# Gates of a two-block transformer kernel: products of two groups of tokens in one go, comparisons issued on their own

## The chip, the cores and the metric

The kernel runs on one core of a Trainium2 chip. The metric is the device time of one execution in microseconds (us), and the time before is the median of three runs. A core has a matrix engine (TensorE, PE in the profile; its weight loads are a row of their own, PEld), a vector engine (VectorE, DVE), an activation engine (ScalarE, ACT), a general engine (GpSimd, POOL) and a queue that issues transfers (SyncE, SP). They run side by side, each through its own instructions in program order, and wait for each other through semaphores.

## The reference

Two transformer blocks run on 256 tokens of width 1024. The change lies in the last part of the second block, a mixture of 16384 very small experts. Per token, 8 heads choose 16 experts each, so 128 experts, with gates from a softmax:

```python
i1 = jnp.take_along_axis(i_top[:, :, 0], c_idx // PEER_TOPK, axis=-1)
i2 = jnp.take_along_axis(i_top[:, :, 1], c_idx % PEER_TOPK, axis=-1)
expert = i1 * N_KEYS + i2
gates = jax.nn.softmax(c_score, axis=-1)
...
a = jax.nn.gelu(jnp.einsum('td,thkd->thk', xb, u).astype(jnp.float32), approximate=False)
w = (gb * a).astype(xb.dtype)
```

An expert is a pair (i1, i2) of 128 keys each. Instead of gathering the rows of the chosen experts, the kernel computes the activation of all 16384 experts for all tokens and multiplies it by a gate that is zero where an expert wasn't chosen. For a token the 128 x 128 gates are the sum over its 128 choices of gate x onehot(i1) x onehot(i2), which is a matrix product with the choices on the contracted axis.

## The kernel before, in words

`Builder` writes the instructions of all engines in one pass. Weights come as 533 units of 128 x 1024 floats (512 KB), each loaded by SP into one of three raw buffers (`load`) and split by `prefetch` into a high part `hi` (ACT, L169) and a rest `lo` (DVE, L170), so that a product takes three matmuls, high by high, high by low and low by high.

The stage concerned is the loop over the 128 units `pu` in `peer`. For each, `f_tile` (L324) makes 24 matmuls of 256 columns into one of two PSUM banks `mm` (lines L332 to L334), with a call of `tick(1.3, False)` after 12 of them and of `tick(1.3)` at the end. Between the last matmul and the second tick it calls the unit's `evac`, `evu`: a gelu on ACT of the tokens whose gates aren't there yet, straight into X (L1488), and for the tokens whose gates are there a gelu on ACT in PSUM (L1490) and a multiplication on DVE into X (L1491), which holds the gates. The second tick also splits one more unit (L169, L170). A bank `mm` is free for the next unit but one when its L1491 is done.

Order of the work around the change: `tick` takes 1.3 from the count of each side task, a Python generator, and runs it on while that count is not positive; what the generator yields is added to the count. `gates` is such a task. A bare yield of it stands for 3.3, so that a group of four tokens falls on every second or third tick. There are 64 groups. For one group `hot` writes, for each of the four tokens, `m1` (a comparison of the row 0 to 127 with the first key of each choice, POOL, L1375), `oh` = `m1` times the gate's high part (ACT, L1377), `m2` = a comparison with the second key, scaled (DVE, L1378) and `ol` = `m1` times the gate's rest (DVE, L1380), all 128 x 128 in half precision; of each of the four tiles there are two buffers. The products are eight matmuls of 128 columns (L1388), per token one with `oh` and one with `ol`, into a PSUM bank `sd`, of which there are two in turn. The spread then takes the bank apart: for the units not yet multiplied (from `u_done` up) ACT copies the gates into X (L1396); for those already there DVE multiplies X by them (L1398), with tokens and units crossed.

In the kernel before, a step of the task issues the products of group g, then `hot(g + 1)`, then the spread of group g, and yields. `routing`, which comes ahead of it in the same task, makes the keys `kT`.

Of the kernel before, what the change touches and what calls it, by code (L numbers as in the profile page):

```python
# [8 lines left out]
F16 = mybir.dt.float16  # L9
I32 = mybir.dt.int32  # L10
U32 = mybir.dt.uint32
AF = mybir.ActivationFunctionType
OP = mybir.AluOpType
# [103 lines left out]
class Builder:  # L117
# [363 lines left out]
    def spread(self, hn, t, dst, col):  # L481
        self.transposes(hn[t].ap, t, dst, col)
        hn[t].free()
# [882 lines left out]
    def gates(self, kT, X):  # L1366

        nc = self.nc

        def hot(g):  # L1370
            tile = lambda name: self.pw.tile([128, 4, 128], F16, name=name, bufs=2)
            m1, m2, oh, ol = (tile(n) for n in ("m1", "m2", "oh", "ol"))
            key = lambda w, i: kT[:, w, 4 * g + i:4 * g + i + 1]
            for i in range(4):
                nc.gpsimd.tensor_scalar(m1[:, i], self.iota, key(0, i), None, op0=OP.is_equal)  # L1375
            for i in range(4):
                nc.scalar.activation(oh[:, i], m1[:, i], AF.Copy, scale=key(2, i))  # L1377
                nc.vector.tensor_scalar(m2[:, i], self.iota, key(1, i), 1.0 / self.SCALE, op0=OP.is_equal, op1=OP.mult)  # L1378
            for i in range(4):
                nc.vector.tensor_scalar(ol[:, i], m1[:, i], key(3, i), None, op0=OP.mult)  # L1380
            return (oh, ol), m2
        o = hot(0)
        yield
        for g in range(64):
            ps = self.sd()
            for i in range(4):
                for p in range(2):
                    nc.tensor.matmul(ps[:, i * 128:i * 128 + 128], o[0][p][:, i], o[1][:, i], start=(p == 0),  # L1388
                                     stop=(p == 1))
            if g < 63:  # L1390
                o = hot(g + 1)
            E = self.u_done
            pv = ps.rearrange("p (t i) -> p t i", t=4)
            x = X[:, :, 4 * g:4 * g + 4].rearrange("p i t -> p t i")
            if E < 128:
                nc.scalar.activation(x[:, :, E:128], pv[:, :, E:128], AF.Copy)  # L1396
            if E:
                nc.vector.tensor_mul(x[:, :, 0:E], pv[:, :, 0:E], x[:, :, 0:E])  # L1398
            self.g_done = 4 * g + 4
            yield  # L1400

    def peer(self):
        nc, hT = self.nc, self.uT
# [407 lines left out]
```

## Time and profile before

| what | us |
|---|---|
| median of 3 runs (lowest to highest) | 1655.06 (1654.47 to 1655.62) |
| the profiled execution, its own time | 1655.53 |
| its span in the profile | 1653.8 |
| PE busy in the span | 1632.5 |
| DVE busy | 1148.0 |
| ACT busy | 977.9 |
| POOL busy | 268.6 |
| POOL's comparisons L1375 alone, 256 of them | 233.2 |

The span is the time between the first and the last event of the profile; the profiled execution's own time has 1.7 us more around it. An engine's busy time is the time in which at least one of its instructions is under way; instructions of one engine overlap a little, so that the distance from one start to the next is often shorter than a duration. POOL's comparisons start between 1003.5 and 1283.9 us; that stretch is Gates.

### The profile page before, as it was taken

How to read it: one execution, taken by the hardware profiler on the slowest of the kernel's cores; microseconds unless marked ns; L12 is line 12 of the kernel's file. 1: busy time of each engine (PE TensorE's matmuls, PEld its weight loads, DVE VectorE, ACT ScalarE, POOL GpSimd, SP SyncE). 2: the span in 40 equal slices, each digit the busy share in tenths (PEclk: the TensorE clock that was granted, in tenths of full speed). 3: DMA queues.
4: the chain of work that ended last, by engine and by line, in shares of the span. 5: the costliest groups of instructions: out<-in, count | busy, mean ns of one | idle time of the engine just before them, and what ended most of it. 6: DMA issues, size and time to landing. Idle time of an engine off the chain costs nothing.

```text
span 1653.8 us, 29236 instructions
## 1 busy us (share of the span) xinstructions
PE 1632.5 (99%) x11102; PEld 1481.6 (90%) x11102; DVE 1148.0 (69%) x2366; ACT 977.9 (59%) x1826; POOL 268.6 (16%) x311
## 2 busy tenths in 40 slices
PE   8999999999999999999999999999999999999998
PEld 6999899988898899979889999999999888888886
DVE  6554765877756645487657998899999755555554
ACT  6443676786555544467355565888877555444454
POOL 0000000000000000000100003988888000000000
PEclk9999999999999999999999999999999999999999
DMA  7565643364524656555244555444454555555553
GB/s 280 192 208 175 227 143 116 115 202 143 179 103 154 216 190 206 177 185 197 78 140 143 192 190 192 166 163 164 161 166 153 180 205 194 194 195 193 191 191 128
DMA packets 79325, 288.77 MB, mean 175 GB/s; under 512 B 8784, under 2 KB 8912, under 8 KB 79056
## 3 DMA queue, kind: packets, MB, share of 16 engines
q1 hardware_dynamic: 77904, 281.66, 49.8%
q10 hardware_dynamic: 1280, 5.24, 1.0%
q8 instruction: 87, 1.43, 0.3%
q14 instruction: 54, 0.44, 0.1%
HBM read 285.82 MB, written 1.05 MB: 173 GB/s over the span
## 4 chain that ended last, share of the span: by engine, by line
PE 81%; DVE 11%; ACT 3%; issue 2%; DMA 2%; POOL 1%; SPq 0%; POOLq 0%; DVEq 0%; ACTq 0%
PE mm L332 12%; PE mm L334 12%; PE mm L333 12%; PE acc L349 10%; PE acc L351 10%; PE acc L353 10%; DVE lo L170 4%; PE mm L303 2%; PE mm L300 2%; PE mm L299 2%; DMA raw<-ws 2%; PE sd L1388 1%; ACT hi L169 1%; DVE m L1378 1%; DVE X L1260 1%
## 5 line engine op out<-in xcount | busy, mean ns | idle before, releaser
L170 DVE TENSOR_TENSOR lo<-raw,hi 128x1024 fp32r<-128x1024 f32 x414 | 506.6, 1228 | 237.5 <-ACT hi L169 236.1
L332 PE MATMUL mm<-uT,hi 128*128 128x256 f32 x2104 | 597.1, 284 | 2.1 <-DVE X L1491 1.7
L334 PE MATMUL mm<-uT,lo 128*128 128x256 f32 x2104 | 587.1, 279 | 0.0
L333 PE MATMUL mm<-uT,hi 128*128 128x256 f32 x2104 | 586.9, 279 | 0.0
L169 ACT ACTIVATE hi<-raw 128x1024 fp32r<-128x1024 f32 x414 | 436.3, 1058 | 214.9 <-PE acc L353 171.1
L332 PEld LDWEIGHTS mm<-uT,hi 128*128 128x128 f32 x2104 | 397.1, 189 | 4.9 <-DVE X L1491 2.6
L333 PEld LDWEIGHTS mm<-uT,hi 128*128 128x128 f32 x2104 | 397.1, 189 | 0.8
L334 PEld LDWEIGHTS mm<-uT,lo 128*128 128x128 f32 x2104 | 397.0, 189 | 0.0
L1375 POOL TENSOR_SCALAR m<-iota,kT 128x128 f16<-128x128 f16 x256 | 233.2, 927 | 197.8 <-DVE kT L1358 149.9
L438 POOL TENSOR_TENSOR hr<-hv,mhalf 128x1 f32<-128x1 f32 x26 | 14.4, 552 | 816.3 <-DVE hv L437 816.3
L349 PE MATMUL acc<-hi,wf 128*128 128x512 f32 x384 | 118.9, 390 | 0.0
L351 PE MATMUL acc<-lo,wf 128*128 128x512 f32 x384 | 118.7, 389 | 0.0
L353 PE MATMUL acc<-hi,wf 128*128 128x512 f32 x384 | 118.5, 389 | 0.0
L170 DVE TENSOR_TENSOR lo<-fa,hi 128x1024 fp32r<-128x1024 f32 x69 | 84.1, 1233 | 34.0 <-ACT hi L169 33.7
L531 ACT ACTIVATE fa<-mm 128x256 f32<-128x256 f32 x36 | 13.8, 383 | 122.9 <-PE mm L334 122.9
L351 PEld LDWEIGHTS acc<-lo,wf 128*128 128x128 f32 x384 | 72.1, 188 | 15.2
L353 PEld LDWEIGHTS acc<-hi,wf 128*128 128x128 f32 x384 | 72.1, 188 | 15.1
L349 PEld LDWEIGHTS acc<-hi,wf 128*128 128x128 f32 x384 | 72.1, 188 | 14.9
L1488 ACT ACTIVATE X<-mm 128x256 f32<-128x256 f32 (+40 forms) x126 | 39.6, 314 | 76.0 <-PE mm L334 75.0
L1377 ACT ACTIVATE oh<-m,kT 128x128 f16<-128x128 f16 x256 | 81.1, 390 | 0.0
L169 ACT ACTIVATE hi<-fa 128x1024 fp32r<-128x1024 f32 x69 | 70.7, 1051 | 5.6 <-PE mm L303 3.1
L1398 DVE TENSOR_TENSOR X<-sd,X 128x184 f32<-128x184 f32 (+31 forms) x64 | 60.9, 951 | 1.2 <-ACT X L1396 1.1
(364 smaller groups left out, 2550.9 us busy)
## 6 DMA issues: line engine op xcount, KB each, us to landing
raw<-ws SPq DMA_DIRECT2D x442, 512.0 KB, 3.3
fa<-ws SPq DMA_DIRECT2D x91, 512.0 KB, 4.4
fa<-rows ACTq DMA_DIRECT2D x5, 512.0 KB, 4.7
fa<-mem ACTq DMA_DIRECT2D x1, 1024.0 KB, 7.7
X<-keysT ACTq DMA_DIRECT2D x1, 1024.0 KB, 5.0
out<-X SPq DMA_DIRECT2D x4, 256.0 KB, 2.0
h<-x SPq DMA_DIRECT2D x2, 256.0 KB, 2.8
h<-x SPq DMA_DIRECT2D x1, 512.0 KB, 7.3
```

The lines of the kernel that those rows point to most:

```text
L169: nc.scalar.activation(hi, raw, AF.Copy)
L170: nc.vector.tensor_sub(lo, raw, hi.bitcast(F32))
L332: nc.tensor.matmul(ps, wh, ah[:, k, :], start=(k == 0), stop=False)
L333: nc.tensor.matmul(ps, wh, al[:, k, :], start=False, stop=False)
L334: nc.tensor.matmul(ps, wl, ah[:, k, :], start=False, stop=(k == 7))
L349: nc.tensor.matmul(o[h], ah[:, k, ts], hi[:, hs[h]], start=first, stop=False)
L351: nc.tensor.matmul(o[h], ah[:, k, ts], lo[:, hs[h]], start=False, stop=False)
L353: nc.tensor.matmul(o[h], al[:, k, ts], hi[:, hs[h]], start=False, stop=last)
L1375: nc.gpsimd.tensor_scalar(m1[:, i], self.iota, key(0, i), None, op0=OP.is_equal)
L1377: nc.scalar.activation(oh[:, i], m1[:, i], AF.Copy, scale=key(2, i))
L1398: nc.vector.tensor_mul(x[:, :, 0:E], pv[:, :, 0:E], x[:, :, 0:E])
L1488: nc.scalar.activation(X[:, i, g:256], ps[:, g:256], AF.Gelu)
```

## The change

The tiles of `hot` are the same, but its comparisons on POOL are a function of their own, `ones`, and the products and the spread of a group too. Two groups are made up at the start. Then a round takes two groups: the 16 matmuls of both, into both banks `sd`; the comparisons of the group after next; a yield of 1.3; the rest of that group's `hot` and the spread of the first group; the comparisons of the next one; a yield of 2.7; the rest of its `hot` and the spread of the second group; a yield of 2.6. The three yields together are 6.6, twice 3.3. The computation is the same.

```diff
-        def hot(g):
-            tile = lambda name: self.pw.tile([128, 4, 128], F16, name=name, bufs=2)
-            m1, m2, oh, ol = (tile(n) for n in ("m1", "m2", "oh", "ol"))
-            key = lambda w, i: kT[:, w, 4 * g + i:4 * g + i + 1]
+        tile = lambda name: self.pw.tile([128, 4, 128], F16, name=name, bufs=2)
+        key = lambda g, w, i: kT[:, w, 4 * g + i:4 * g + i + 1]
+
+        def ones(g):
+            m1 = tile("m1")
             for i in range(4):
-                nc.gpsimd.tensor_scalar(m1[:, i], self.iota, key(0, i), None, op0=OP.is_equal)
+                nc.gpsimd.tensor_scalar(m1[:, i], self.iota, key(g, 0, i), None, op0=OP.is_equal)
+            return m1
+
+        def hot(g, m1):
+            m2, oh, ol = (tile(n) for n in ("m2", "oh", "ol"))
             for i in range(4):
...
             return (oh, ol), m2
-        o = hot(0)
-        yield
-        for g in range(64):
+
+        def products(o):
             ps = self.sd()
             for i in range(4):
                 for p in range(2):
...
-            if g < 63:
-                o = hot(g + 1)
+            return ps
+
+        def spread(g, ps):
             E = self.u_done
...
             self.g_done = 4 * g + 4
-            yield
+        o = [hot(g, ones(g)) for g in range(2)]
+        yield
+        for g in range(0, 64, 2):
+            pss = [products(p) for p in o]
+            o = []
+            for i in range(2):
+                more = g + 2 + i < 64
+                if more:
+                    m1 = ones(g + 2 + i)
+                yield 1.3 if i == 0 else 2.7
+                if more:
+                    o.append(hot(g + 2 + i, m1))
+                spread(g + i, pss[i])
+            yield 2.6
```

## Rows read from the trace of the kernel before

**Rows 1.** The page: the span, and busy us (share) and instructions of each engine.

```profile
span 1653.8 us, 29236 instructions
PE 1632.5 (99%) x11102; PEld 1481.6 (90%) x11102; DVE 1148.0 (69%) x2366; ACT 977.9 (59%) x1826; POOL 268.6 (16%) x311
```

**Rows 2.** Three stretches: length, then PE, PEld, DVE, ACT, POOL busy; clock; DMA.

```profile
1028.00:1100.00 72.00, 72.00 (x678) 71.25 (x678) 64.83 (x198) 63.14 (x155) 65.58 (x72) 1.00 0.47 160
1100.00:1200.00 100.00, 100.00 (x939) 99.01 (x937) 97.81 (x286) 82.87 (x214) 86.55 (x98) 1.00 0.49 164
1200.00:1291.00 91.00, 89.56 (x821) 86.88 (x821) 91.00 (x243) 68.12 (x186) 71.12 (x80) 1.00 0.46 156
```

**Rows 3.** Waits, 1028 to 1292 us: us in total, times, longest us.

```profile
POOL m L1375 <- DVE ol L1380: 44.0, 46, 14.6
...
PEld mm L332 <- DVE X L1491: 2.6, 5, 0.7
...
PEld L1388 <- DVE ol L1380: 0.3, 1, 0.3
```

**Rows 4.** PE in order of time, around 1147 us: start us, duration us.

```profile
1143.31 0.23 PE L1388 MATMUL sd<-m,oh 128*128 128x128 f16 x1
...
1146.65 0.23 PE L1388 MATMUL sd<-m,oh 128*128 128x128 f16 x1
...
1147.05 0.22 PE L1388 MATMUL sd<-m,ol 128*128 128x128 f16 x1
1147.08 0.36 PE L332 MATMUL mm<-uT,hi 128*128 128x256 f32 x1
...
1151.41 0.23 PE L1388 MATMUL sd<-m,oh 128*128 128x128 f16 x1
```

**Rows 5.** DVE in order of time, around 1149 us.

```profile
1147.06 0.26 DVE L1491 TENSOR_TENSOR X<-X,mm 128x116 f32<-128x116 f32 x1
1147.25 1.27 DVE L170 TENSOR_TENSOR lo<-raw,hi 128x1024 fp32r<-128x1024 f32 x1
1148.45 0.84 DVE L1378 TENSOR_SCALAR m<-iota,kT 128x128 f16<-128x128 f16 x4
...
1149.90 0.92 DVE L1398 TENSOR_TENSOR X<-sd,X 128x328 f32<-128x328 f32 x1
1150.74 0.26 DVE L1491 TENSOR_TENSOR X<-X,mm 128x120 f32<-128x120 f32 x1
```

**Rows 6.** A unit's last matmul and its L1491, in order of time.

```profile
1122.26 0.28 PE L334 MATMUL mm<-uT,lo 128*128 128x256 f32 x1
...
1123.18 0.25 DVE L1491 TENSOR_TENSOR X<-X,mm 128x92 f32<-128x92 f32 x1 [0.38 <-ACT mm L1490]
```

**Rows 7.** DVE in order of time, around 1258 us.

```profile
1256.37 0.37 DVE L1491 TENSOR_TENSOR X<-X,mm 128x220 f32<-128x220 f32 x1
1256.66 1.22 DVE L170 TENSOR_TENSOR lo<-raw,hi 128x1024 fp32r<-128x1024 f32 x1
1257.80 0.86 DVE L1378 TENSOR_SCALAR m<-iota,kT 128x128 f16<-128x128 f16 x4
...
1259.29 1.21 DVE L1398 TENSOR_TENSOR X<-sd,X 128x460 f32<-128x460 f32 x1
1260.40 0.39 DVE L1491 TENSOR_TENSOR X<-X,mm 128x224 f32<-128x224 f32 x1
```

**Rows 8.** PE in order of time: first products of two groups, four groups apart.

```profile
1251.32 0.23 PE L1388 MATMUL sd<-m,oh 128*128 128x128 f16 x1
...
1268.53 0.23 PE L1388 MATMUL sd<-m,oh 128*128 128x128 f16 x1
```

**Rows 9.** DVE in order of time, around 1039 us.

```profile
1038.10 0.85 DVE L1378 TENSOR_SCALAR m<-iota,kT 128x128 f16<-128x128 f16 x4
...
1040.08 0.16 DVE L1491 TENSOR_TENSOR X<-X,mm 128x12 f32<-128x12 f32 x1
```

**Rows 10.** Line L1375: duration ns least/median/most, first and last start us.

```profile
L1375 POOL TENSOR_SCALAR m<-iota,kT x256: 595/681/2586, 1003.5 to 1283.9; 128x128 f16<-128x128 f16 x128
```

More of the change, by code (lines that the diff above doesn't have):

```diff
@@ L1368, in gates @@
         nc = self.nc
-        def hot(g):
-            tile = lambda name: self.pw.tile([128, 4, 128], F16, name=name, bufs=2)
-            m1, m2, oh, ol = (tile(n) for n in ("m1", "m2", "oh", "ol"))
-            key = lambda w, i: kT[:, w, 4 * g + i:4 * g + i + 1]
+        tile = lambda name: self.pw.tile([128, 4, 128], F16, name=name, bufs=2)
+        key = lambda g, w, i: kT[:, w, 4 * g + i:4 * g + i + 1]
+        def ones(g):
+            m1 = tile("m1")
             for i in range(4):
-                nc.gpsimd.tensor_scalar(m1[:, i], self.iota, key(0, i), None, op0=OP.is_equal)
+                nc.gpsimd.tensor_scalar(m1[:, i], self.iota, key(g, 0, i), None, op0=OP.is_equal)
+            return m1
+        def hot(g, m1):
+            m2, oh, ol = (tile(n) for n in ("m2", "oh", "ol"))
             for i in range(4):
-                nc.scalar.activation(oh[:, i], m1[:, i], AF.Copy, scale=key(2, i))
-                nc.vector.tensor_scalar(m2[:, i], self.iota, key(1, i), 1.0 / self.SCALE, op0=OP.is_equal, op1=OP.mult)
+                nc.scalar.activation(oh[:, i], m1[:, i], AF.Copy, scale=key(g, 2, i))
+                nc.vector.tensor_scalar(m2[:, i], self.iota, key(g, 1, i), 1.0 / self.SCALE, op0=OP.is_equal, op1=OP.mult)
             for i in range(4):
-                nc.vector.tensor_scalar(ol[:, i], m1[:, i], key(3, i), None, op0=OP.mult)
+                nc.vector.tensor_scalar(ol[:, i], m1[:, i], key(g, 3, i), None, op0=OP.mult)
             return (oh, ol), m2
-        o = hot(0)
-        yield
-        for g in range(64):
+        def products(o):
             ps = self.sd()
@@ L1388, in gates @@
                     nc.tensor.matmul(ps[:, i * 128:i * 128 + 128], o[0][p][:, i], o[1][:, i], start=(p == 0),
-                                     stop=(p == 1))
-            if g < 63:
-                o = hot(g + 1)
+                                    stop=(p == 1))
+            return ps
+        def spread(g, ps):
             E = self.u_done
```

## The prediction

> **What bounds the kernel now.** I read the page first: TensorE (PE) is busy for 1632.5 of 1653.8 us [rows 1], so a change tells only where it makes PE wait or gives PE less to do. The diff touches one stretch, the 64 groups of Gates, so the second view is the table of busy time over that stretch [rows 2]: 1028 to 1291 us, granted clock 1.00 throughout. PE is busy for all of it until 1200, and loses 1.4 us after. VectorE (DVE) is nearly as full: 64.8 of 72, then 97.8 of 100, then 91.0 of 91 us. So PE bounds the first two thirds, both together the last, and DVE has almost nothing spare anywhere. The reader should see that a shift in order which leaves DVE idle for a microsecond is paid for by PE.
>
> Third, the waits of the stretch [rows 3]: PE waited 2.6 us at its weight loads for DVE's L1491 (a PSUM bank of the unit products came back late), and only 0.3 us at the one-hot products, for `ol`. No row names a wait of a product for the spread L1398. That wait exists in the code (the bank must be read before it is written again), and it never ended last.
>
> Fourth, the order in time. Products start at 1143.31, 1146.65 and 1151.41 [rows 4]: gaps of 3.34 and 4.76 us, alternately two and three ticks of 12 unit matmuls. So a tick takes 4.76 - 3.34 = 1.42 us, one group's products 3.34 - 2.84 = 0.50 us, and four groups 2 x (3.34 + 4.76) = 16.2 us. Of the 0.50, the eight matmuls take 0.43 (1146.65 to 1147.08); 0.07 is what going over and back costs.
>
> **The change, part by part.**
>
> *Fewer switches.* 16 products in one go instead of twice 8: 32 times 0.07 us = 2.2 us less PE work, if PE has nothing else to wait for. That is the whole direct gain.
>
> *Comparisons issued apart.* POOL's queue holds nothing but these in the stretch, in the same order before and after. It already runs ahead: it waited 44.0 us in 46 places for `ol` [rows 3], which is the release of the `m1` buffer (two exist), and no row has ACT's `oh` waiting for POOL. An instruction issued earlier in program order still waits for that buffer. I cost this part at nothing; its cover is that lead, and losing it is rival C. SP's loads are issued by the unit loop as before; if PE slows, they are wanted later, not earlier.
>
> *The banks.* This is the step that decides. A pair takes 6.6 of the scheduler's time: products of both groups; 1.3 later (one tick) B = `hot(g+2)`, spread of g; 2.7 later (two ticks, one time in 13 three) C = `hot(g+3)`, spread of g+1; 2.6 later (two ticks) the next products. There are two `sd` banks. Before, a bank alternated: group g's spread was issued with g, its bank wanted again two groups, five ticks, later. Now the second bank is wanted two ticks after C, plus the first group's 0.43 us: 2 x 1.42 + 0.43 = 3.27 us. How long does DVE take from such an issue to the end of its spread? The group at 1146.65 was issued through at 1147.08 [rows 4]; its spread started at 1149.90 and took 0.92, so it ended at 1150.82 [rows 5], 3.74 us after. That is already over 3.27. So PE will wait in front of the second group's products, and so behind it the unit matmuls, whose `evac` DVE needs next.
>
> The Trainium skill, PSUM — Partial Sum Buffer, section "PSUM bank collisions raise a hardware error", has the rule that PSUM is to be guarded by bank, not by address, so the products may not start while the spread still reads. By it the sum is the one below; without it only the 2.2 us would be left, and the time would fall. No row before shows this wait, so the trace neither bears it out nor contradicts it.
>
> *What it costs.* Once PE waits for it each pair, the end of C's spread sets the pace. Let s be that end. DVE's chain from s to the next such end has two forms, since a pair takes five ticks and a unit has two (middle and end).
> Middle case (products amid a unit): second group and switch 0.50, half a unit 1.42, then from the unit's last matmul to its L1491 0.92 (1122.26 to 1123.18 [rows 6]) less the 0.12 that this matmul lies before the half unit's end: 2.72. Then L1491, B, L170, L1491, C.
> End case (products at a unit's end): DVE alone: three L170, two L1491, B, C. PE's own least is 5 x 1.42 + 0.93 = 8.03.
>
> Around group 29 [rows 5]: L1491 0.19 (1147.06 to 1147.25), one B or C 2.29 (1148.45 to 1150.74), the tail of the spread beyond its successor's start 0.08; L170 1.14 (1256.66 to 1257.80 [rows 7], same shape). Middle: 2.72 + 0.38 + 1.14 + 4.58 + 0.08 = 8.90. End: 3.42 + 0.38 + 4.58 = 8.38. Four groups: 17.28 against 16.20: **+1.08**.
> Around group 56 [rows 7]: L1491 0.29, step 2.60, tail 0.10. Middle: 2.72 + 0.58 + 1.14 + 5.20 + 0.10 = 9.74. End: 3.42 + 0.58 + 5.20 = 9.20. Together 18.94, against the 17.21 that four groups took (1251.32 to 1268.53 [rows 8]): **+1.73**.
> Around group 2 [rows 9]: step 1.98, L1491 some 0.1. Middle 8.12, end 7.58, which PE's 8.03 covers: 16.15 against 16.20: **0**.
> The middle case is the dear one: DVE idles until the unit's L1491 is ready, with B queued behind it, where the old order had a group's work ready there.
> The loss per four groups grows about evenly from 0 at group 2 over 1.08 at group 29 to 1.73 at group 56: 27/4 x 0.54 + 27/4 x 1.40 + 8/4 x 1.75 = 3.6 + 9.5 + 3.5 = **16.6 us**. The switches' 2.2 us are in it already (0.93 for a pair).
>
> What is not in the trace: how late the bank wait makes things when ACT, which must finish `oh` and its part of the spread first, is late too. Least: only the DVE-bound last third pays, 22/4 x 1.7 = 9, less 1.5 for the 21 switches of the first 42 groups: +8. Most: 1.73 in all sixteen stretches, +28. I take the middle, which the rows at three places give. At the end nothing changes: two units' work followed the last products, and its spread comes at most a tick later.
>
> The sum stands against the profiled execution's 1655.5 us (span 1653.8): 1672.1. The median is 0.5 lower, so 1671.6, **1672 us**.
>
> **Rivals.**
>
> *B, PE stays the bound, not slower.* If DVE ended C's spread within 3.27 us, no wait arises and the 2.2 us are saved; if the order also cured the late evacuations, 2.6 us more [rows 3]. So 1650 to 1653. For it: PE is fully busy until 1200, and the unit work between is unchanged. Against it: 3.74 us where 3.27 is needed, at a place where DVE was not yet full; it decides where B and C together cost DVE less than about 4.0 us, which rows 9 show only at the start.
>
> *C, POOL becomes the bound.* POOL is busy for 223 of 263 us [rows 2], and single comparisons run from 595 to 2586 ns [rows 10]. If each group pays 4 x 0.917 and a full wait of 44.0/46 = 0.96 for its buffer, a pair takes 9.26 against 8.2: 32 x 1.06 = +34, 1689 us. For it: POOL's lead shrinks if `ol` comes in clusters. Against it: a slower pair also gives POOL longer, and its waits now are slack.
> The Trainium skill, SBUF — State Buffer, section "Who interferes with whom", says that a DVE operation in a two-port mode and a GpSimd operation shut each other out for a whole instruction. By that rule two closer DVE steps would stretch the comparisons in this way; the spread of 595 to 2586 ns agrees, but the rule doesn't say how often.
>
> That the comparisons' half of the change does nothing is part of every case, as worked out above.
>
> **How the numbers follow.** Forecast 0.75, B 0.20, C 0.05. A measurement of this kernel can tell about 0.2%, 3.3 us, from no change. Of B, 0.12 lies within that and 0.08 is faster by more (it needs the 2.6 us and the upper price of a switch). So faster 0.08, same 0.12, slower 0.80. The range takes in +8 and, from +28, all but the last microseconds, and reaches down into B's upper part: 1654 to 1682.
>
> **What would show it.** In the changed profile: a new wait of L1388 for DVE's L1398 (some 15 us or more, half of the pairs at the least, the ninth product of a go late); DVE with idle time before L1491 in every second pair; four groups at 17.3 us in the middle; the last product some 17 us later against the first. The forecast is wrong if L1388 doesn't wait, if the first third pays as much as the last (then ACT's chain sets the pace), or if `oh` waits for POOL (C).

## The result and the profile after

The changed kernel takes 1675.21 us (median of 4 runs, 1674.83 to 1676.47), the kernel before in the same comparison 1655.34: 19.9 us more, a ratio of 1.012 with an interval of 1.0107 to 1.0133. The forecast was 1672, its range 1654 to 1682. The profiled execution of the changed kernel took 1676.47 us, 1.3 more than its median, with a span of 1674.7.

First the table of busy time, over nearly the same stretches as [rows 2], with the same columns (length; PE, PEld, DVE, ACT, POOL busy; clock; DMA share; GB/s):

```profile
1028.00:1100.00 72.00, 68.36 (x641) 66.95 (x640) 61.19 (x201) 57.50 (x144) 59.48 (x69) 1.00 0.46 151
1100.00:1200.00 100.00, 93.49 (x873) 91.72 (x873) 89.39 (x259) 76.29 (x202) 81.81 (x91) 1.00 0.46 153
1200.00:1300.00 100.00, 89.18 (x834) 87.41 (x833) 91.71 (x252) 70.11 (x193) 77.80 (x89) 1.00 0.44 147
```

Before, PE was busy for all of the first two stretches and DVE for all of the last. Now no engine is full anywhere: PE lacks 3.6, 6.5 and 10.8 us, and DVE lacks 10.8, 10.6 and 8.3. The two that were full before now both stand idle in part; the next rows show that each waits for the other, DVE by way of ACT. The granted clock is the same, 1.00 in every stretch.

The waits of the stretch, 1028 to 1315 us (who waited for whom: us in total, times, longest us), answer to [rows 3]:

```profile
POOL m L1376 <- DVE ol L1385: 34.9, 35, 2.2
PEld L1392 <- issue: 25.6, 31, 1.7
DVE X L1509 <- ACT mm L1508: 24.5, 17, 1.6
PE sd L1392 <- DVE X L1403: 21.1, 30, 1.5
...
ACT oh L1382 <- POOL m L1376: 1.7, 2, 1.5
```

L1392 is the products, L1403 DVE's part of the spread, L1509 the unit's multiplication (L1388, L1398 and L1491 before). A wait that no row of before had, of the products for the spread, stands there 30 times, in all but one of the 31 pairs that follow another (that one pauses at its ninth product too, 0.7 us that the view puts down to ACT's L1508); the weight loads show the same pauses as "issue" and aren't to be added. The other new one is DVE's wait for the unit's gelu, 24.5 us in 17 places, about every second pair, against 3.3 us before. The late evacuations of [rows 3], 2.6 us, are gone: PE now stops earlier.

One pair in order of time, DVE and PE of the changed kernel around 1160 us (start us, duration us, idle time before in brackets):

```profile
1156.16 0.27 DVE L1509 TENSOR_TENSOR X<-X,mm 128x112 f32<-128x112 f32 x1 [1.46 <-ACT mm L1508]
1156.35 0.73 DVE L1383 TENSOR_SCALAR m<-iota,kT 128x128 f16<-128x128 f16 x4
...
1157.73 0.94 DVE L1403 TENSOR_TENSOR X<-sd,X 128x328 f32<-128x328 f32 x1
1158.58 1.34 DVE L170 TENSOR_TENSOR lo<-raw,hi 128x1024 fp32r<-128x1024 f32 x1
1159.85 0.26 DVE L1509 TENSOR_TENSOR X<-X,mm 128x116 f32<-128x116 f32 x1
1160.04 0.73 DVE L1383 TENSOR_SCALAR m<-iota,kT 128x128 f16<-128x128 f16 x4
1160.69 0.77 DVE L1385 TENSOR_SCALAR ol<-m,kT 128x128 f16<-128x128 f16 x4
1161.38 0.87 DVE L1403 TENSOR_TENSOR X<-sd,X 128x332 f32<-128x332 f32 x1
```

```profile
1161.01 0.23 PE L1392 MATMUL sd<-m,oh 128*128 128x128 f16 x1
...
1161.41 0.22 PE L1392 MATMUL sd<-m,ol 128*128 128x128 f16 x1
1162.30 0.22 PE L1392 MATMUL sd<-m,oh 128*128 128x128 f16 x1 [0.66 <-DVE X L1403]
```

The eight products of the first group run from 1161.01; the ninth needs the second bank, whose spread ends at 1161.38 + 0.87 = 1162.25, and starts 0.05 us after. Upwards in DVE's rows stands where the delay of this pair comes from: DVE did nothing for 1.46 us until the unit's L1509 was ready at 1156.16, and the step B that it could have done meanwhile stands behind that instruction in its queue. From there on it works without a gap through B, L170, L1509 and C, and is late.

Where the 20.9 us between the two profiled executions lie: 2.1 were there before the first product (1030.59 against 1028.52), and belong to the executions and not to the change (the variant e4 below, which issues the same work up to there, has its first product at 1028.75). From the first product to the end it is 644.1 against 625.3, so 18.8 us. The first products of every tenth pair cut the stretch (PE in order of time, changed kernel):

```profile
1030.59 0.23 PE L1392 MATMUL sd<-m,oh 128*128 128x128 f16 x1
...
1116.16 0.23 PE L1392 MATMUL sd<-m,oh 128*128 128x128 f16 x1
...
1205.10 0.23 PE L1392 MATMUL sd<-m,oh 128*128 128x128 f16 x1
...
1307.00 0.23 PE L1392 MATMUL sd<-m,oh 128*128 128x128 f16 x1
```

In the kernel before the same groups (0, 20, 40 and 62) began at 1028.52, 1109.55, 1192.06 and 1285.91. So the first ten pairs took 85.6 instead of 81.0 (+4.5), the next ten 88.9 instead of 82.5 (+6.4), the last eleven 101.9 instead of 93.9 (+8.0).

### The profile page after: what moved, and what is told of

Its sections match the earlier page's. It is cut to its first block, busy times and chain, and to the rows that moved or that the text cites. A ratio compares the mean times of both kernels' runs of the same rounds, so it can differ in the third digit from the quotient of the medians.

```text
span 1674.7 us, 29251 instructions
## 1 busy us (share of the span) xinstructions
PE 1631.9 (97%) x11102; PEld 1480.5 (88%) x11102; DVE 1144.8 (68%) x2366; ACT 972.7 (58%) x1826; POOL 267.5 (16%) x311
## 4 chain that ended last, share of the span: by engine, by line
PE 78%; DVE 11%; ACT 5%; issue 3%; DMA 1%; POOL 1%; SPq 0%; POOLq 0%; ACTq 0%; DVEq 0%
PE mm L332 12%; PE mm L334 11%; PE mm L333 11%; PE acc L349 10%; PE acc L351 10%; PE acc L353 10%; DVE lo L170 4%; PE mm L303 2%; PE mm L300 2%; PE mm L299 2%; ACT hi L169 2%; DVE m L1383 2%; DVE X L1403 1%; DVE ol L1385 1%; DMA raw<-ws 1%
## 5 line engine op out<-in xcount | busy, mean ns | idle before, releaser
L170 DVE TENSOR_TENSOR lo<-raw,hi 128x1024 fp32r<-128x1024 f32 x414 | 505.7, 1226 | 238.2 <-ACT hi L169 237.0
L170 DVE TENSOR_TENSOR lo<-fa,hi 128x1024 fp32r<-128x1024 f32 x69 | 83.9, 1230 | 34.0 <-ACT hi L169 33.7
L1403 DVE TENSOR_TENSOR X<-sd,X 128x184 f32<-128x184 f32 (+31 forms) x64 | 59.9, 936 | 1.7 <-ACT X L1401 1.5
```

Of the source, the lines that this page charges most:

```text
L170: nc.vector.tensor_sub(lo, raw, hi.bitcast(F32))
```

## The experiments

**Four variants of the changed kernel.** The first moves both steps, B and C, one tick nearer to the products before them, so that three ticks instead of two lie behind C; the pairs stay.

```diff
                 if more:
                     m1 = ones(g + 2 + i)
-                yield 1.3 if i == 0 else 2.7
+                if i == 1:
+                    yield 2.6
                 if more:
                     o.append(hot(g + 2 + i, m1))
                 spread(g + i, pss[i])
-            yield 2.6
+            yield 4.0
```

> Edit: the products stay in pairs and the comparisons stay apart, but the first group's hot and spread follow the products at once, the second group's come two ticks later (2.6), and the next products three ticks after that (4.0); the sum of the yields stays 6.6. Theory (the second bank's spread comes too late, because only two ticks lie between its issue and the next products): now 3 x 1.42 + 0.43 = 4.69 us lie between, more than the 3.7 that DVE needs in the middle of the stretch and about what it needs at its end, so the wait of the products for the spread falls from 21 us to under 5 and the time comes to 1654 to 1660. Rival (two groups in one go cost by themselves, through POOL or through DVE's bunched work): 1670 to 1677.

Measured: 1652.88 us (10 runs), a ratio of 0.9984 (0.9974 to 0.9993) to the kernel before. The whole loss is gone, and 2.7 us more. The table of its stretches:

```profile
1028.00:1100.00 72.00, 72.00 (x687) 71.65 (x686) 68.42 (x214) 62.96 (x158) 66.20 (x78) 1.00 0.49 163
1100.00:1200.00 100.00, 100.00 (x957) 99.37 (x957) 98.65 (x282) 83.75 (x220) 88.84 (x99) 1.00 0.49 164
1200.00:1300.00 100.00, 97.16 (x870) 94.25 (x869) 98.31 (x247) 72.01 (x189) 65.75 (x74) 1.00 0.49 163
```

PE is full again until 1200, with 957 matmuls in the 100 us where the kernel before had 939. The products of e1 wait for the spread hardly at all:

```profile
PE sd L1392 <- DVE X L1403: 0.4, 2, 0.2
```

So the pairs as such cost nothing; the place of the steps between them did. The gain of 2.7 us (1.1 to 4.3 by the interval) agrees with the 2.2 us that the prediction put on fewer switches. Up to 1190 us the median time from a first product to the second unit matmul after the products is 0.63 us for the eight products of before and 1.08 for the sixteen of e1. Twice the one, less the other and less one matmul of 0.12, is the 0.07 us per pair that the prediction took. The rest of the gain isn't accounted for.

The second leaves the order alone and takes away one thing that the products wait for.

```diff
             if E:
+                if g % 2:
+                    pv = kT[:, :, 0:128]
                 nc.vector.tensor_mul(x[:, :, 0:E], pv[:, :, 0:E], x[:, :, 0:E])
```

> Edit: in the changed kernel DVE's part of the spread of every second group (the odd ones) multiplies X by kT, in SBUF, instead of by the bank, so the gates of these tokens aren't the reference's in the units already there. DVE has the same number of instructions, but the second bank is released by ACT alone. Theory (the products wait for DVE's read of the second bank): what remains to wait for is ol of the same group, which ends one spread earlier (0.6 to 1.2 us, about the size of the wait), so most of the 20 us go: 1655 to 1662. Rival (bank not the cause; DVE's idle time in every second pair or POOL is): stays within 4 us of the changed kernel, 1671 to 1677.

Measured: 1656.94 us (1.0008, 0.9999 to 1.0018). 18 of the 20 us are gone, though DVE does the same number of instructions of the same length (its groups over the stretch, 32 of each kind: busy us, mean ns):

```profile
L1405 DVE TENSOR_TENSOR X<-kT,X 128x188 f32<-128x188 f32 (+31 forms) x32 | 30.6, 955 | 0.0
L1405 DVE TENSOR_TENSOR X<-sd,X 128x184 f32<-128x184 f32 (+31 forms) x32 | 30.6, 955 | 1.4 <-ACT X L1401 1.1
```

The control, the same edit in the kernel before:

> Edit: the same as in e2_other_source, in the kernel before: DVE's part of the spread of every second group multiplies X by kT instead of by the bank, so the gates of these tokens aren't the reference's in the units already there. It tells what the other source is worth by itself. Theory: there no product waits for the spread, so only a change of DVE's or POOL's durations could show: 1653 to 1657. Rival (the other source is itself what made e2_other_source 18 us shorter than the changed kernel): 1640 or less.

Measured: 1656.42 us (1.0006, 0.9997 to 1.0016). The other source by itself gains nothing; what it removed from the changed kernel is the wait for the bank. With it went most of DVE's wait for the gelu, 6.6 us in 10 places instead of 24.5 in 17, although the order of DVE's queue is the same: that idle time mostly followed from the late products.

The third asks whether it is the bank alone.

```diff
-                if more:
-                    o.append(hot(g + 2 + i, m1))
                 spread(g + i, pss[i])
+                if more:
+                    o.append(hot(g + 2 + i, m1))
```

> Edit: in the changed kernel's steps B and C the spread is issued ahead of hot instead of behind it. Theory (a step of DVE issued two ticks before its result is needed): the bank comes back 1.4 us earlier, but ol, which the same go of products needs, ends as late as the spread did, so the wait changes its name and not its length: 1671 to 1678, products waiting for L1385 (ol). Rival (the bank alone matters): the wait goes, 1654 to 1661.

Measured: 1667.08 us (1.0069, 1.0052 to 1.0086): outside both. 8.1 us came back, and 11.5 stayed over the 1655.59 of the kernel before in that comparison. The waits of the stretch:

```profile
PEld L1392 <- DVE ol L1385: 14.3, 23, 1.2
...
PE sd L1392 <- DVE ol L1385: 7.8, 18, 0.7
```

The wait did change its name: it is `ol` now, and no row has the products waiting for the spread. But it became shorter, which the expectation had not seen. Every second product needs one of the four `ol`, and the ninth to sixteenth follow them one by one, while the spread is a single instruction that must end. In the pair at 1152.83 us, for instance, the ninth product starts at once, the tenth 0.51 us after it, and the fourteenth and sixteenth come 0.22 and 0.17 after the product before them. So the limit is the step C issued two ticks ahead; which of its instructions ends last sets how much it costs.

The fourth undoes the other half of the change.

```diff
-                if more:
-                    m1 = ones(g + 2 + i)
                 yield 1.3 if i == 0 else 2.7
                 if more:
-                    o.append(hot(g + 2 + i, m1))
+                    o.append(hot(g + 2 + i, ones(g + 2 + i)))
```

> Edit: in the changed kernel the comparisons are issued again together with the rest of hot, right before it. Theory: POOL's queue holds the same comparisons in the same order and starts each when its buffer is free, so nothing changes: within 2 us of the changed kernel, 1673 to 1677. Rival (issuing them apart is part of the loss, or of a gain): off by more than 4 us either way.

Measured: 1674.8 us, against 1675.21. Its products wait 19.5 us for the spread, as in the changed kernel (21.1).

**The distance the other way, and the parts alone.** One tick instead of two:

```diff
-                yield 1.3 if i == 0 else 2.7
+                yield 1.3 if i == 0 else 4.0
...
-            yield 2.6
+            yield 1.3
```

> Edit: in the changed kernel the yields are 1.3, 4.0 and 1.3 instead of 1.3, 2.7 and 2.6, so that the second group's hot and spread come one tick ahead of the next products instead of two. Theory: 1.42 + 0.43 = 1.85 us lie between, against 3.27, so the products wait longer for the spread; but DVE, which has idle time in every second pair, then starts the second group's work that much nearer to its data, so that not all of the 1.42 us per pair (45 us) comes on top. From the chain (products 0.50, four ticks 5.68, the unit's evacuation 0.80, L1491 and one step of DVE 2.3) a pair takes 9.3 to 9.6 instead of 8.8: 1690 to 1705 us. Rival (the distance isn't the cause): within 4 us of the changed kernel, 1671 to 1679.

Measured: 1711.67 us (1.0342, 1.0326 to 1.0358), 36.5 more than the changed kernel, or 1.14 of the 1.42 us per pair. The direction is right and the size above the range: only 0.28 us of the later tick is hidden, less than the expectation's chain had it.

```profile
DVE X L1509 <- ACT mm L1508: 48.7, 45, 2.1
PE sd L1392 <- DVE X L1403: 47.7, 28, 2.7
```

With three, two and one ticks between C and the next products the time is 1652.9, 1675.2 and 1711.7, and the wait for the spread 0.4, 21.1 and 47.7 us.

The comparisons apart, in the order of the kernel before:

```diff
-        o = hot(0)
+        o = hot(0, ones(0))
+        m1 = ones(1)
...
             if g < 63:
-                o = hot(g + 1)
+                o = hot(g + 1, m1)
+            if g < 62:
+                m1 = ones(g + 2)
```

> Edit: the kernel before with only the comparisons apart: one group at a time as before, and the comparisons of the group after next are issued a step ahead of the rest of its hot. Theory: POOL starts each comparison when its buffer is free, wherever it was issued, so nothing changes: 1654 to 1657. Rival (apart is worth something by itself): under 1652 or over 1659.

Measured: 1655.78 us (1.0002, 0.9993 to 1.0012). Together with e4, both ways round: this half of the change does nothing that these runs can tell.

And `hot` two groups ahead, one group at a time:

```diff
+        o = [hot(g, ones(g)) for g in range(2)]
...
-            if g < 63:
-                o = hot(g + 1)
+            if g < 62:
+                o.append(hot(g + 2, ones(g + 2)))
```

> Edit: one group at a time, as before, but hot runs two groups ahead of the products instead of one, as at the start of the changed kernel. The bank keeps its five ticks. Theory: the products never waited for ol before (0.3 us), so a longer lead of hot alone gains nothing, and DVE's work is the same: 1653 to 1658. Rival (the loss came with the second set of hot made ahead, from the buffers or the start): 1662 or more.

Measured: 1654.96 us (0.9997, 0.9988 to 1.0006). Nothing, as expected: the products had waited only 0.3 us for `ol` before [rows 3].

**What the first third adds.** The forecast had nearly no loss there, and 4.5 us were found.

```diff
             for i in range(4):
-                nc.scalar.activation(oh[:, i], m1[:, i], AF.Copy, scale=key(g, 2, i))
+                if g >= 20 or i == 0:
+                    nc.scalar.activation(oh[:, i], m1[:, i], AF.Copy, scale=key(g, 2, i))
...
```

> What is open: the first ten pairs of the changed kernel take 8.56 us each, where the prediction's chain through DVE gave 8.03 to 8.1 there. Edit: in the changed kernel ACT makes only one of the four oh of each group below 20, and that group's products all read this one, so ACT has 3 x 0.29 = 0.88 us less per group there and three of four tokens of these groups get gates that aren't the reference's; DVE, PE and POOL have the same instructions. Theory (ACT's oh, ahead of its part of the spread and of hi, makes DVE late in the first third): the first ten pairs fall from 85.6 to 81 to 83 us and the time to 1671 to 1673. Rival (DVE's own work is the chain there too): the pairs stay within 1 us, 1674 to 1677.

Measured: 1672.19 us (1.01, 1.0083 to 1.0117), 3.0 less than the changed kernel. The first ten pairs (PE in order of time):

```profile
1029.66 0.23 PE L1393 MATMUL sd<-m,oh 128*128 128x128 f16 x1
...
1111.81 0.23 PE L1393 MATMUL sd<-m,oh 128*128 128x128 f16 x1
```

82.15 us instead of 85.57, with 1.0 us of waiting for the spread instead of 4.2. So 3.4 of the 4.5 us came from ACT's work for `oh`, in a stretch where DVE's own work left it some room (64.8 of 72 us busy before [rows 2]).

Where the forecast had exactly nothing, at groups 2 to 5, the loss is as large as anywhere. The first products of groups 2 and 6 in the changed kernel:

```profile
1038.74 0.23 PE L1392 MATMUL sd<-m,oh 128*128 128x128 f16 x1
...
1056.75 0.23 PE L1392 MATMUL sd<-m,oh 128*128 128x128 f16 x1
```

These four groups took 18.01 us; in the kernel before they took 16.16 (1036.63 to 1052.79), and in e9 16.23 (1037.80 to 1054.03). The rows of ACT and DVE in between show the chain in the open:

```profile
1043.08 0.16 ACT L1508 ACTIVATE mm<-mm 128x8 f32<-128x8 f32 x1
1043.15 1.27 ACT L1382 ACTIVATE oh<-m,kT 128x128 f16<-128x128 f16 x4
1044.32 0.74 ACT L1401 ACTIVATE X<-sd 128x316 f32<-128x316 f32 x1
...
1045.10 0.63 DVE L1403 TENSOR_TENSOR X<-sd,X 128x196 f32<-128x196 f32 x1 [0.34 <-ACT X L1401]
1045.96 1.23 DVE L170 TENSOR_TENSOR lo<-raw,hi 128x1024 fp32r<-128x1024 f32 x1 [0.23 <-ACT hi L169]
```

ACT makes the four `oh` and then its part of the spread; DVE's part waits for that, and the next L170 for the `hi` behind it. From there DVE runs without a gap to C's spread, for which the ninth product of the next pair waits 0.65 us.

**A version that beats both.** `e1_lead` has its only loss of PE time in the last third, where DVE is 98% busy and PE at 97. ACT has room there. On top of e1's order:

```diff
             for i in range(4):
-                nc.vector.tensor_scalar(ol[:, i], m1[:, i], key(g, 3, i), None, op0=OP.mult)
+                if i == 3 and g >= 40:
+                    nc.scalar.activation(ol[:, i], m1[:, i], AF.Copy, scale=key(g, 3, i))
+                else:
+                    nc.vector.tensor_scalar(ol[:, i], m1[:, i], key(g, 3, i), None, op0=OP.mult)
...
```

> Edit: e1_lead, and from group 40 on one of the four ol of a group is made by ACT instead of by DVE. Theory (in the last third DVE is full, 98 to 100% in e1_lead, and PE waits some 5 us for its L1491 there): 24 x 0.17 = 4 us less on DVE, of which PE gets back 2 to 4: 1648.5 to 1651. Rival (ACT's chain of oh and its part of the spread is what is late there): no gain, or up to 3 us more than e1_lead, 1652 to 1656.

Measured: 1649.01 us (5 runs, 1648.71 to 1650.0), 0.9965 (0.9952 to 0.9979) of the kernel before, 6.3 us less. The last stretch of its table:

```profile
1200.00:1300.00 100.00, 99.41 (x885) 96.93 (x884) 96.06 (x224) 78.98 (x211) 64.96 (x72) 1.00 0.51 169
```

PE is back at 99%, DVE has 96 instead of 98, and ACT, at 79 instead of 72, still has room.

## Why the prediction was right

**The bound** was read rightly for the last two thirds: both PE and DVE without anything spare, so that a shift in order which idles DVE is paid for by PE. That is the 24.5 us of DVE behind L1509 beside the 21.1 us of PE behind the spread. "Almost nothing spare anywhere" went too far for the first third, where DVE was busy for 90%. And DVE's idle time isn't the price by itself: in the first ten pairs it is 7.7 us behind the gelu in e9 as in the changed kernel, where the products wait 1.0 and 4.2 us.

**The banks**, the step that was to decide, decided. It stood on one comparison: 3.27 us from C's issue to the need, 3.74 us from such an issue to the end of its spread in [rows 4, 5]. The ninth product waits, as said; e1 (4.69 us, 0.4 us of waiting in all), e2 (another source, no wait for the spread) and e5 (1.85 us, more than twice the wait) show that this is the cause; e3 adds that with the bank back sooner `ol` of the same step takes over part of the wait. The prediction rested the wait on the rule of the Trainium skill (PSUM — Partial Sum Buffer, "PSUM bank collisions raise a hardware error") that PSUM is to be guarded by bank, not by address. The trace agrees as far as it goes: the products pause 0.66 us at the start of the second bank and not at the first. It can't tell the two ways of guarding apart, because the products overwrite the very addresses that the spread reads; so "without it only the 2.2 us would be left" doesn't follow, and the wait would be there with a guard by address too.

**The chain in two forms.** The first products of groups 28 and 32 in the changed kernel:

```profile
1152.41 0.23 PE L1392 MATMUL sd<-m,oh 128*128 128x128 f16 x1
...
1169.75 0.23 PE L1392 MATMUL sd<-m,oh 128*128 128x128 f16 x1
```

These four groups took 17.34 us, against the 17.28 worked out, and those from group 56 on 18.52 (1278.74 to 1297.26) against 18.94. The middle case showed DVE idle ahead of L1509 in about every second pair, as said. Around group 2, where 16.20 was the forecast, it was 18.01.

**The sum**, 16.6, is 18.8 in the profiled executions. The term that was too small is the first third: from 0 at group 2, the even growth gave 1.6 us up to group 20, and 4.5 were paid. The sentence that failed is "PE's 8.03 covers" the chain there: it followed DVE alone, though the paragraph on what the trace does not show had named ACT's `oh` and its part of the spread as the unknown. e9 puts 3.4 of these us on ACT. The middle ten pairs cost 6.4 against 5.4, the last eleven 8.0 against 8.8, and from group 62 to the end the time is the same (367.9 before, 367.7 after), so the errors partly cancel. By its own signs the prediction was half warned: it called itself wrong if the first third paid as much as the last, and per pair the thirds paid 0.45, 0.64 and 0.73 us. Another sign, the last product some 17 us later against the first, came out at 15.5; pairing moves the last group's products 3.5 us nearer to those of group 62, which the sign had left out.

**The comparisons' half at nothing** holds (e4, e6). **Fewer switches** at 2.2 us agrees with e1: hidden in the changed kernel, and part of the 2.7 us gained once the order lets PE be the bound.

**The rivals.** B, PE stays the bound and nothing is lost, would have been right with three ticks instead of two: e1 is that case, at the upper end of its 1650 to 1653. C, POOL as the bound, fell: `oh` waited for POOL 1.7 us in all, and POOL stood idle more than before: 65.4 us in front of its comparisons (the row of the last section) against 47.9.

```profile
L1375 POOL TENSOR_SCALAR m<-iota,kT 128x128 f16<-128x128 f16 x248 | 223.3, 917 | 47.9 <-DVE ol L1380 44.0 <-ACT X L1396 1.4 <-ACT oh L1377 1.0
```

The price of +34 was also worked out from a mean that isn't typical: of the 44.0 us in 46 places [rows 3], 14.6 are a single wait ahead of 1027.96 us, which the changed kernel has too. The other 45 are 0.65 us each, and with that the same sum gives +14.

## What to carry to other kernels

When work is batched into several buffers that used to alternate, count for each buffer the time from the issue of its last reader to its next writer, before and after: here the batch took five ticks down to two for one bank, and the wait that came of it cost 20 us, where the batching itself was worth some 2 us. In a queue worked in order, look for an instruction that waits for another engine and stands ahead of work that is ready and on somebody's path, as L1509 stood ahead of B; no run here changed that by itself. A walk through such a queue has to follow every engine of the chain, not only the busiest two: here it was ACT, at 88% in the first third [rows 2].

## What the runs showed of the hardware that was not expected

With DVE's spread of every second group reading kT from SBUF instead of a PSUM bank, POOL's comparisons grew, though DVE's instructions kept their length (e2_other_source, then the changed kernel; busy us, mean ns | idle before):

```profile
L1376 POOL TENSOR_SCALAR m<-iota,kT 128x128 f16<-128x128 f16 x248 | 244.6, 1004 | 27.0 <-DVE m L1383 14.6 <-DVE ol L1385 9.5 <-ACT X L1401 1.7
```

```profile
L1376 POOL TENSOR_SCALAR m<-iota,kT 128x128 f16<-128x128 f16 x248 | 221.6, 911 | 65.4 <-DVE ol L1385 34.9 <-DVE m L1383 14.6 <-ACT X L1401 6.4
```

That is 23 us over 248 comparisons, for 32 instructions of DVE with 30.6 us in all, and the control in the kernel before shows the same (1012 ns against 917). The Trainium skill, SBUF — State Buffer, section "Who interferes with whom", says that a DVE instruction with both inputs in SBUF contends with a GpSimd instruction that reads SBUF; the rows agree. Both kernels have such an instruction in any case, L170: of the changed kernel's 248 comparisons, the 123 that ran beside an L170 for more than 0.1 us took 1.23 us on average, the 123 that met none 0.64 (a longer one is also likelier to meet one). Here a multiplication that read its second operand from PSUM spared POOL this.
